# The opening of a two-layer trunk: the norm's row by a shuffle, weights ahead of tile two, tile two by VectorE, values ahead of keys

## The chip, the cores and the metric

The kernel runs on one core of one Trainium2 chip. The core has a matrix engine (TensorE, PE in the profile; its weight loads are PEld), a vector engine (VectorE, DVE), a scalar engine (ScalarE, ACT), GpSimd (POOL) and a sync engine (SyncE, SP) that here only issues loads and stores. PE writes into PSUM, everything else lies in SBUF, the on-chip memory, with 128 partitions. The metric is the device time of one execution in microseconds; the median over runs is what is compared.

## The reference

Two residual layers, each with one RMS norm, one wide input projection, three parallel token mixers (a Mamba-2 scan, sliding-window attention with sinks, forgetting attention) and one output projection, on 256 tokens of width 1024, all in float32. What matters here is how a layer begins:

```python
def rms_norm(x, w):
    xf = x.astype(jnp.float32)
    y = xf * lax.rsqrt(jnp.mean(xf * xf, axis=-1, keepdims=True) + NORM_EPS)
    return (y * w.astype(jnp.float32)).astype(x.dtype)
...
        h = rms_norm(x, norm_w[layer])
        proj = jnp.einsum('bsd,de->bse', h, w_in[layer])
...
    q = rope(q.reshape(b, s, SWA_HEADS, HEAD_DIM), cos, sin)
    k = rope(k.reshape(b, s, SWA_KV_HEADS, HEAD_DIM), cos, sin)
    v = v.reshape(b, s, SWA_KV_HEADS, HEAD_DIM)
```

The norm's weight `norm_w` is one row of 1024 numbers that multiplies every token. The first columns that the kernel projects are the 256 of the sliding window's keys (`b_k`) and the 256 of its values (`b_v`).

## The kernel before

**Tiling.** The 256 tokens are two tiles of 128 rows ("tile one" and "tile two"). A projection multiplies the transposed normalized tokens by a weight piece of 256 or 512 columns; the width of 1024 is cut into eight steps `k` of 128. To keep float32 accuracy with fast matmuls, each operand is split into a rounded part `hi` and a remainder `lo`, and each step is three matmuls: hi by hi, remainder of the tokens by hi, tokens by lo. So one tile by one piece is 24 matmuls.

**Weights.** SP loads the weights in parts of 512 KB into six buffers `raw` (`load_to`, line 345). ACT copies a part to `hi` (line 268, in the opening line 1209), then DVE subtracts to get `lo` (line 269; in the opening line 1210, where each part is done in two halves and POOL does the second half). A `raw` buffer is free for the next load once its `lo` is made; `hi` and `lo` have six buffers each and come free when PE has used the part. A 256-column piece is two parts, a 512-column piece four.

**The opening** is written out by hand in the first `manual_schedule` block, where each engine runs its instructions in program order. PE does 30 warm-up transposes. For each tile the sum of squares is built from two halves, `row_var` and `rsqrt` make the inverse root on DVE with one power on POOL (line 207), and the scaled row `h` is transposed by PE, four 128x128 blocks to a half, and split into `hTh` and `hTl` (`to_hT`). Tile one is scaled by DVE (line 1221). Tile two is multiplied by the norm's weight on POOL (1223, 1229) and by its inverse root on ACT (1235, 1237). Its transposes stand between the halves of the first 24 matmuls (`second_rows`). Then come keys of tile two, values of tile one, values of tile two (`u_bkv`): in all 96 matmuls of 256 columns. After a keys' unit DVE applies rope in three steps (474, 476, 477), POOL makes two sums (496), and a later step `rest` has PE transpose them and ACT evacuate (504).

**What follows** is written in an order that a planner sets from estimated PE time: the queries' piece of 512 columns for both tiles (`u_bq`, POOL's sums at line 517), a small piece, gate columns, and so on. `launch` gives a step a due time, and `pump`, called in the middle and at the end of units, issues the steps that are due. `layer_consts` issues nine small loads from ACT's queue (line 263): three into `vr`, four into `hb`, and two into `dsk` that gather `d_skip` element by element. SP and ACT loads share eight completion semaphores in turn, so a load can also wait for the load that last used its semaphore.

## Time and profile before

| what | value |
|---|---|
| median of 3 runs | 840.53 us (840.38 to 842.8) |
| profiled execution | 841.65 us |
| its span, first to last instruction | 839.8 us |
| mean granted TensorE clock | 0.997 |
| PE busy | 822.7 us, 98% of the span |
| loads: HBM read | 155.22 MB |

The span is what the profile covers; the execution's own time is 1.85 us longer. Rows of the profile give the start in microseconds, the duration, the engine, the line of the kernel, and the tiles written and read. A bracket at the end of a row is idle time of that engine just before it, with what ended the idle time. "ACTq" and "SPq" are the issuing of loads on those engines.

### The profile page before, as it was taken

The numbers are of one execution on the slowest core, as the hardware profiler recorded it, in microseconds if no ns is written. First come the engines' busy times: TensorE is split into PE (matmuls) and PEld (weight loads), VectorE is DVE, ScalarE is ACT, GpSimd is POOL, SyncE is SP. The second block draws the span as 40 slices with busy tenths as digits, with TensorE's granted clock in tenths as the row PEclk, the third lists the DMA queues.
The fourth block names the chain that finished last, engine by engine and source line by source line (L and its number), as shares of the span: only waits on it lengthen the run. The fifth ranks groups of instructions, "written<-read, shape, count | busy, mean of one in ns | idle before, by whom it ended". The sixth has DMA issues, their size and how long they took to land.

```text
span 839.8 us, 15652 instructions
## 1 busy us (share of the span) xinstructions
PE 822.7 (98%) x5800; PEld 749.8 (89%) x5800; DVE 655.9 (78%) x1355; ACT 503.3 (60%) x970; POOL 123.4 (15%) x167
## 2 busy tenths in 40 slices
PE   7999999999999999999999999999999999999996
PEld 6989888989989998888989998898899999888896
DVE  5778997998776678876688879979968668788665
ACT  6466777665556675544455668775556667655442
POOL 7411400000211101110014122000003110211000
PEclk9999999999999999999999999999999999999999
DMA  9576565567456546776577455556756564576632
GB/s 304 163 228 201 177 201 164 173 216 226 140 156 212 177 149 189 232 218 215 191 225 242 143 184 171 161 188 211 229 173 181 172 178 150 177 221 216 213 102 74
DMA packets 123595, 158.39 MB, mean 189 GB/s; under 512 B 12784, under 2 KB 84192, under 8 KB 123520
## 3 DMA queue, kind: packets, MB, share of 16 engines
q1 hardware_dynamic: 109456, 140.79, 53.9%
q10 hardware_dynamic: 14016, 16.49, 6.4%
q8 instruction: 45, 0.74, 0.4%
q14 instruction: 30, 0.25, 0.1%
q0 software_dynamic: 48, 0.13, 0.0%
HBM read 155.22 MB, written 2.16 MB: 187 GB/s over the span
## 4 chain that ended last, share of the span: by engine, by line
PE 82%; DVE 7%; DMA 4%; ACT 3%; issue 2%; POOL 1%; ACTq 1%; SPq 0%; POOLq 0%; DVEq 0%
PE mm L97 70%; PE mx L97 9%; DMA raw<-in_w_in_dram 4%; PE mx L101 3%; DVE lo L269 3%; ACT hi L268 1%; POOL sm L858 1%; DVE L L836 1%; DVE L L837 1%; DVE pp L577 1%; DVE pp L559 0%; ACT L L845 0%; ACTq L263 0%; ACT pp L565 0%; DVE L L842 0%
## 5 line engine op out<-in xcount | busy, mean ns | idle before, releaser
L269 DVE TENSOR_TENSOR lo<-raw,hi 128x1024 fp32r<-128x1024 f32 x252 | 310.8, 1247 | 77.4 <-ACT hi L268 71.9
L97 PE MATMUL mm<-hi,L 128*128 128x512 f32 (+1 forms) x1280 | 354.0, 363 | 1.8 <-ACT hi L1209 1.2
L97 PE MATMUL mm<-L,hi 128*128 128x256 f32 x1792 | 318.4, 279 | 0.9 <-DVE L L477 0.9
L268 ACT ACTIVATE hi<-raw 128x1024 fp32r<-128x1024 f32 x252 | 263.3, 1055 | 90.0 <-PE mm L97 68.3
L97 PEld LDWEIGHTS mm<-L,hi 128*128 128x128 f32 x1792 | 278.8, 193 | 6.9 <-issue 3.2
L97 PEld LDWEIGHTS mm<-hi,L 128*128 128x128 f32 x1280 | 229.2, 190 | 30.6 <-issue 2.4
L97 PE MATMUL mm<-L,lo 128*128 128x256 f32 x896 | 247.4, 276 | 0.0
L97 PE MATMUL mm<-lo,L 128*128 128x512 f32 (+1 forms) x640 | 229.4, 359 | 1.4 <-POOL lo L1210 1.4
L97 PEld LDWEIGHTS mm<-L,lo 128*128 128x128 f32 x896 | 172.7, 193 | 0.2
L97 PEld LDWEIGHTS mm<-lo,L 128*128 128x128 f32 x640 | 120.9, 189 | 15.4 <-POOL lo L1210 1.8
L908 POOL TENSOR_SCALAR_AFFINE_SELECT bias<-bias 128x128 f32<-128x128 f32 x64 | 37.3, 614 | 265.4 <-DMA bias<-cumd 265.3
L768 DVE SCALAR_TENSOR_TENSOR L<-L,vec,L 128x255 f32<-128x255 f32 (+2 forms) x96 | 46.9, 489 | 6.1 <-ACT L L765 4.8
L97 PE MATMUL mx<-L,L 128*64 128x128 f32 (+1 forms) x384 | 36.5, 332 | 0.0
L640 ACT ACTIVATE pp<-pp,nm 128x128 f32<-128x128 f32 x64 | 25.2, 394 | 15.6 <-DVE nm L633 12.6
L97 PEld LDWEIGHTS mx<-L,L 128*64 128x64 f32 x384 | 23.8, 137 | 11.9 <-issue 2.7
L565 ACT ACTIVATE pp<-pp,nm 128x128 f32<-128x128 f32 x64 | 28.2, 442 | 7.2 <-DVE nm L559 7.2
L932 ACT ACTIVATE L<-L 128x512 f32<-128x512 f32 x24 | 15.1, 627 | 29.0 <-DVE L L931 28.7
L829 ACT ACTIVATE L<-mm 128x256 f32<-128x256 f32 x48 | 18.0, 375 | 21.1 <-PE mm L97 17.4
L771 ACT ACTIVATE L<-L 128x256 f32<-128x256 f32 x32 | 13.4, 418 | 27.3 <-DVE L L768 26.9
L665 POOL TENSOR_SCALAR_AFFINE_SELECT L<-L 128x256 f32<-128x256 f32 x16 | 10.9, 680 | 107.7 <-ACT L L663 107.7
L633 DVE CUSTOM_DVE_ANT_0 pp<-mx,wmask,nsink 128x128 f32<-128x128 f32 x64 | 24.2, 413 | 1.8 <-PE mx L97 1.8
L858 POOL TENSOR_TENSOR sm<-sm,mhalf 128x4 f32<-128x4 f32 x8 | 10.9, 1363 | 91.8 <-DVE sm L855 91.8
(181 smaller groups left out, 820.8 us busy)
## 6 DMA issues: line engine op xcount, KB each, us to landing
raw<-in_w_in_dram SPq DMA_DIRECT2D x200, 512.0 KB, 4.7
raw<-in_w_proj_dram SPq DMA_DIRECT2D x48, 512.0 KB, 4.6
raw<-in_w_out_dram SPq DMA_DIRECT2D x16, 512.0 KB, 4.8
...
bias<-cumd ACTq DMA_DIRECT2D x16, 256.0 KB, 3.7
L<-in_gate_bias_dram ACTq DMA_DIRECT2D x12, 256.0 KB, 3.6
...
```

What stands on the lines that cost most here:

```text
L97: nc.tensor.matmul(o, a, b, **kw)
L101: nc.tensor.transpose(o, a, i)
L268: keep(act)(hi, src, AF.Copy)
L269: keep(tt)(lo, src, hi.bitcast(F32), op=ALU.subtract)
L565: act(pp[:, i, sl], pp[:, i, sl], AF.Exp, scale=-1.0, bias=nm[:, e:e + 1], accum_out=sums[:, e:e + 1])
L633: nc.vector.tensor_tensor_reduce(out=pp[:, i, sl], in0=score(p, i, b), in1=m, scale=-0.125, scalar=ns[:, i:i + 1], op0=ALU.add, op1=ALU.mi ...
L640: act(pp[:, i, sl], pp[:, i, sl], AF.Exp, scale=-1.0, bias=nm[:, e:e + 1], accum_out=sums[:, e:e + 1])
L768: stt(a[:, s:S], x_[:, 0:S - s], y.vec[:, 16 * j + u:16 * j + u + 1], a[:, s:S], op0=ALU.mult, op1=ALU.add)
L829: act(halves(th), p, AF.Tanh, scale=0.5)
L858: nc.gpsimd.tensor_tensor(r0[:, 0:4], v[:, 0:4], mhalf[:, 0:4], op=ALU.pow)
L908: nc.gpsimd.affine_select(out=bias[:, i, dst], in_=bias[:, i, src], compare_op=ALU.is_ge, fill=NEG, base=0, pattern=[[-1, P]], channel_mul ...
L932: act(g, g, AF.Tanh, scale=0.5)
```

## The change

Four things are changed, all in the opening.

- **The norm's row.** Before, SP loaded `norm_w` into all 128 partitions (512 KB). Now DVE clears a tile `nwr`, ACT issues a load of the row into four partitions (0, 32, 64 and 96; 16 KB), and two DVE shuffles spread partition 0 of each group of 32 over its group, into `nwb0`.
- **First weights ahead of tile two.** SP's order of loads was tile one, norm's weight, tile two, weights. It is now tile one, the first weight part, tile two, the other weights.
- **Tile two by DVE.** DVE now takes half of tile two's squares, and scales it in one step as it does tile one; both tiles are scaled in place. The POOL products and ACT scalings go. The inverse root is shorter by two DVE steps (`first_root`, `last_root`), and the first weight part's `lo` is made by DVE alone.
- **Values of tile one ahead of keys of tile two.** PE's order of units was keys one, keys two, values one, values two; it is keys one, values one, keys two, values two. Tile two's transposes now stand after keys one and in the middle of values one.

From there on the order on all engines is the same but for a few steps of the planner that move by some rows. The places of which the prediction speaks, as the instructions stand in program order:

On DVE, the first instructions before (ss is the sum of squares, sm and rs the small columns of the inverse root, L_22 the scaled tile one):

```order
L158 MEMSET tab_63 128x1
L1215 ISA L_26_154,ss_148<-L_2_66 128x512
L1215 ISA ss_148 128x1
L223 TENSOR_REDUCE sm_158<-ss_148 128x1
L224 TENSOR_SCALAR sm_158<-sm_158 128x1
L209 TENSOR_TENSOR sm_163<-sm_161 128x1
L210 TENSOR_TENSOR sm_163<-sm_163,sm_158 128x1
L211 TENSOR_SCALAR sm_163<-sm_163 128x1
L213 TENSOR_TENSOR rs_167<-sm_161,sm_163 128x1
L1221 SCALAR_TENSOR_TENSOR L_22_150<-L_2_66,rs_167,nwb_67 128x512 x2
```

And now (L_3 is the row's tile `nwr`, L_1 is x):

```order
L161 MEMSET L_3_66 128x1024
L164 MEMSET tab_69 128x1
L1252 STREAM_SHUFFLE nwb_64<-L_3_66 128x512 x2
L1226 ISA L_25_154,ss_150<-L_1_63 128x512
L1226 ISA ss_150 128x1
L241 TENSOR_SCALAR sm_160<-ss_150 128x1
L249 SCALAR_TENSOR_TENSOR sm_164<-sm_162,sm_160 128x1
L250 TENSOR_SCALAR sm_164<-sm_164 128x1
L252 TENSOR_TENSOR rs_167<-sm_162,sm_164 128x1
L1249 SCALAR_TENSOR_TENSOR L_1_63<-L_1_63,rs_167,nwb_64 128x512 x2
```

The shuffles, which read the loaded row, stand ahead of the squares of x; two of the small steps are gone.

On POOL, from the first power on, before (lo_237 and lo_262 are the values' weights, L_54 the sums of the rotated keys):

```order
L207 TENSOR_TENSOR sm_161<-sm_158,mhalf_96 128x1
L1223 TENSOR_TENSOR L_23_151<-L_2_66,nwb_67 128x512
L207 TENSOR_TENSOR sm_186<-sm_176,mhalf_96 128x1
L1210 TENSOR_TENSOR lo_195<-raw_105,hi_194 128x512
L1229 TENSOR_TENSOR L_23_151<-L_2_66,nwb_67 128x512
L1210 TENSOR_TENSOR lo_210<-raw_107,hi_209 128x512
L1210 TENSOR_TENSOR lo_237<-raw_109,hi_236 128x512
L1210 TENSOR_TENSOR lo_262<-raw_111,hi_261 128x512
L496 TENSOR_TENSOR L_54_273<-L_52_268,L_53_270 128x4x64 x2
```

And now (lo_229 and lo_233 are the values' weights):

```order
L243 TENSOR_TENSOR sm_162<-sm_160,mhalf_97 128x1
L243 TENSOR_TENSOR sm_193<-sm_191,mhalf_97 128x1
L1237 TENSOR_TENSOR lo_196<-raw_109,hi_195 128x512
L1237 TENSOR_TENSOR lo_229<-raw_111,hi_228 128x512
L511 TENSOR_TENSOR L_53_263<-L_51_258,L_52_260 128x4x64 x2
L1237 TENSOR_TENSOR lo_233<-raw_113,hi_232 128x512
L511 TENSOR_TENSOR L_59_331<-L_57_326,L_58_328 128x4x64 x2
```

The second half of the values' weights (lo_233) now stands behind the first keys' two sums; before, all weights' remainders stood ahead of them.

On PE, from tile one's last transposes to the first matmul of tile two's keys, before (L_24 and L_25 are hTh and hTl; hi_194 and hi_209 the keys' weights; mm_216 keys of tile one, mm_276 keys of tile two):

```order
L101 MATMUL mx_200<-ident_71,L_22_150 128x128 x4
L97 MATMUL mm_216<-hi_194,L_24_152 128x256 x4
L97 MATMUL mm_216<-hi_194,L_25_153 128x256 x4
L97 MATMUL mm_216<-lo_195,L_24_152 128x256 x4
L101 MATMUL mx_229<-ident_71,L_23_151 128x128 x4
L97 MATMUL mm_216<-hi_209,L_24_152 128x256 x4
L97 MATMUL mm_216<-hi_209,L_25_153 128x256 x4
L97 MATMUL mm_216<-lo_210,L_24_152 128x256 x4
L101 MATMUL mx_254<-ident_71,L_23_151 128x128 x4
L97 MATMUL mm_276<-hi_194,L_24_152 128x256
```

And now, from the second half of tile one's keys to the same place (L_23 and L_24 are hTh and hTl; hi_195 and lo_196 the keys' weights, hi_228, hi_232 and their lo the values'; mm_211 keys of tile one, mm_266 values of tile one, mm_301 keys of tile two):

```order
L97 MATMUL mm_211<-hi_195,L_23_152 128x256 x4
L97 MATMUL mm_211<-hi_195,L_24_153 128x256 x4
L97 MATMUL mm_211<-lo_196,L_23_152 128x256 x4
L101 MATMUL mx_248<-ident_72,L_1_63 128x128 x4
L97 MATMUL mm_266<-hi_228,L_23_152 128x256 x4
L97 MATMUL mm_266<-hi_228,L_24_153 128x256 x4
L97 MATMUL mm_266<-lo_229,L_23_152 128x256 x4
L101 MATMUL mx_279<-ident_72,L_1_63 128x128 x4
L97 MATMUL mm_266<-hi_232,L_23_152 128x256 x4
L97 MATMUL mm_266<-hi_232,L_24_153 128x256 x4
L97 MATMUL mm_266<-lo_233,L_23_152 128x256 x4
L97 MATMUL mm_301<-hi_169,L_23_152 128x256
```

Tile two's transposes (mx_248, mx_279) stand later, and the values' remainder lo_233 is needed ahead of the second tile's keys. On ACT the nine small loads of `layer_consts` stand right behind the evacuation of the first keys' transposes, in both kernels; the semaphores on which they and SP's weight loads wait are others.

The diff, without empty lines:

```diff
--- before.py
+++ after.py
@@ -154,14 +154,15 @@
             print("drained", br, left, "at", round(clock["t"], 1))
+    x0 = T("L8", [P, 2, D])
+    nwb0 = T("nwb", [P, D])
+    nc.sync.dma_start(x0[:, 0, :], x2[0:P, :])
+    nwr = T("L4", [P, D])
+    nc.vector.memset(nwr, 0.0)
+    nc.scalar.dma_start(nwr.rearrange("(a b) d -> a b d", b=32)[:, 0, :], norm_w[0:1, :].to_broadcast([4, D]))
     tab = T("tab", [P, 1])
     nc.vector.memset(tab, 0.0)
     act(tab, tab, AF.Exp)
-    x0 = T("L8", [P, 2, D])
-    nwb0 = T("nwb", [P, D])
-    nc.sync.dma_start(x0[:, 0, :], x2[0:P, :])
-    nc.sync.dma_start(nwb0, norm_w[0:1, :].to_broadcast([P, D]))
-    nc.sync.dma_start(x0[:, 1, :], x2[P:S, :])
     ident = T("ident", [P, P])
     make_identity(nc, ident)
     tri = T("tri", [P, P])
@@ -234,8 +235,22 @@
         stt(r[:, 0:1], a[:, 0:1], -3.0, r0[:, 0:1], op0=ALU.add, op1=ALU.mult)
         return r
-    def row_rstd(ss, n):
-        return rsqrt(row_var(ss, n), 1)
+    def first_root(ss):
+        v = T("sm", [P, 8])
+        ts(v[:, 0:1], ss[:, 0:1], ss[:, 1:2], 1.0 / D, op0=ALU.add, op1=ALU.mult)
+        r0 = T("sm", [P, 8])
+        nc.gpsimd.tensor_tensor(r0[:, 0:1], v[:, 0:1], mhalf[:, 0:1], op=ALU.pow)
+        return v, r0
+    def last_root(v, r0):
+        a = T("sm", [P, 8])
+        stt(a[:, 0:1], r0[:, 0:1], v[:, 0:1], r0[:, 0:1], op0=ALU.mult, op1=ALU.mult)
+        ts(a[:, 0:1], a[:, 0:1], -0.5, 1.5, op0=ALU.mult, op1=ALU.add)
+        r = T("rs", [P, 8], bufs=4)
+        tt(r[:, 0:1], r0[:, 0:1], a[:, 0:1], op=ALU.mult)
+        return r
@@ -1078,6 +1093,7 @@
             pump()
     fin = {}
+    between = []
     def hT(y, t):
         if t == 0:
@@ -1137,9 +1153,9 @@
         if l == 0:
             k, v = cols(C_BK), cols(C_BV)
-            op(k, u_bkv(y, 0, 0, [lambda j=j: second_rows(j) for j in range(2)]))
+            op(k, u_bkv(y, 0, 0, [lambda j=j: between[j]() for j in range(2)]))
             op(k, u_bkv(y, 0, 1))
-            op(v, u_bkv(y, 256, 0), u_bkv(y, 256, 1))
+            op(v, u_bkv(y, 256, 0, [lambda j=j: between[2 + j]() for j in range(2)]), u_bkv(y, 256, 1))
             op(None, lambda: layer_consts(y0))
             for c in (0, 2):
                 op(cols(C_BQ + 256 * c, 512), u_bq(y, c, 0), u_bq(y, c, 1))
@@ -1193,55 +1209,99 @@
     ENG = mybir.EngineType
     with tc.manual_schedule(engines={ENG.PE, ENG.DVE, ENG.Activation, ENG.Pool}):
+        load_to(1)
+        nc.sync.dma_start(x0[:, 1, :], x2[P:S, :])
         load_to(N_RAW)
         warm = pmx()
         for i in range(WARM):
             transpose(warm[:, 0:P], ident, ident)
         ss = [T("ss", [P, 4], bufs=4) for _ in range(2)]
-        h = [T("L4", [P, D]) for _ in range(2)]
         y0.hTh = T("L8", [P, NK // 2, 2, 2 * P], F32R)
         y0.hTl = T("L8", [P, NK // 2, 2, 2 * P], F32R)
-        def shared():
-            for _ in range(2):
-                raw, hi, lo = new_part()
-                for k, sub_ in ((0, tt), (2, gtt)):
-                    ks = slice(k, k + 2)
-                    act(hi[:, ks, :], raw[:, ks, :], AF.Copy)
-                    sub_(lo[:, ks, :], raw[:, ks, :], hi[:, ks, :].bitcast(F32), op=ALU.subtract)
-                yield
-        w0, w1 = shared(), shared()
         half = (slice(0, 512), slice(512, D))
         junk = T("L2", [P, 512])
-        nc.vector.tensor_tensor_reduce(out=junk, in0=x0[:, 0, half[1]], in1=x0[:, 0, half[1]], scale=1.0,
-                                       scalar=0.0, op0=ALU.mult, op1=ALU.add, accum_out=ss[0][:, 1:2])
-        sum_sq(x0, 0, 0, ss[0][:, 0:1], 512)
-        r0 = row_rstd(ss[0], 2)
-        sum_sq(x0, 1, 0, ss[1][:, 0:1], 512)
+        def squares(t):
+            sum_sq(x0, t, 0, ss[t][:, 0:1], 512)
+            nc.vector.tensor_tensor_reduce(out=junk, in0=x0[:, t, half[1]], in1=x0[:, t, half[1]], scale=1.0,
+                                           scalar=D * EPS, op0=ALU.mult, op1=ALU.add,
+                                           accum_out=ss[t][:, 1:2])
+        def part():
+            raw, hi, lo = new_part()
+            def high(k):
+                act(hi[:, k:k + 2, :], raw[:, k:k + 2, :], AF.Copy)
+            def low(k, sub_):
+                sub_(lo[:, k:k + 2, :], raw[:, k:k + 2, :], hi[:, k:k + 2, :].bitcast(F32), op=ALU.subtract)
+            return high, low
+        def turned(t, j):
+            p = pmx()
+            for k in range(4):
+                transpose(p[:, k * P:(k + 1) * P], x0[:, t, j * 512 + k * P:j * 512 + (k + 1) * P], ident)
+            pv = p.rearrange("p (a t) -> p a t", a=2)
+            h, l = y0.hTh[:, 2 * j:2 * j + 2, t, :], y0.hTl[:, 2 * j:2 * j + 2, t, :]
+            return (lambda: act(h, pv, AF.Copy)), (lambda: tt(l, pv, h.bitcast(F32), op=ALU.subtract))
+        def scaled(t, j, r):
+            stt(x0[:, t, half[j]], x0[:, t, half[j]], r[:, 0:1], y0.nwb[:, half[j]], op0=ALU.mult, op1=ALU.mult)
         for sl in half:
-            stt(h[0][:, sl], x0[:, 0, sl], r0[:, 0:1], y0.nwb[:, sl], op0=ALU.mult, op1=ALU.mult)
-        sum_sq(x0, 1, 512, ss[1][:, 1:2], 512)
-        gtt(h[1][:, half[0]], x0[:, 1, half[0]], y0.nwb[:, half[0]], op=ALU.mult)
-        v1 = row_var(ss[1], 2)
-        to_hT(h[0], 0, y0.hTh, y0.hTl, (0,))
-        r1 = rsqrt(v1, 1)
-        next(w0)
-        to_hT(h[0], 0, y0.hTh, y0.hTl, (1,))
-        gtt(h[1][:, half[1]], x0[:, 1, half[1]], y0.nwb[:, half[1]], op=ALU.mult)
-        def second_rows(j):
-            with tc.high_priority():
-                to_hT(h[1], 1, y0.hTh, y0.hTl, (j,))
-            next(w1)
-        act(h[1][:, half[0]], h[1][:, half[0]], AF.Copy, scale=r1[:, 0:1])
-        next(w0)
-        act(h[1][:, half[1]], h[1][:, half[1]], AF.Copy, scale=r1[:, 0:1])
-        for i, f, _ in ops[:2]:
-            f(pieces[i])
+            nc.vector.stream_shuffle(nwb0[:, sl], nwr[:, sl], [0] * 32)
+        squares(0)
+        r0 = last_root(*first_root(ss[0]))
+        h0, l0 = part()
+        h0(0)
+        h0(2)
+        scaled(0, 0, r0)
+        th0, tl0 = turned(0, 0)
+        scaled(0, 1, r0)
+        th0()
+        squares(1)
+        tl0()
+        th1, tl1 = turned(0, 1)
+        l0(0, tt)
+        root = first_root(ss[1])
+        h1, l1 = part()
+        h1(0)
+        th1()
+        h1(2)
+        l0(2, tt)
+        tl1()
+        r1 = last_root(*root)
+        l1(0, tt)
+        l1(2, gtt)
+        scaled(1, 0, r1)
+        scaled(1, 1, r1)
+        k0, k1, v0 = [f for _, f, _ in ops[:3]]
+        low = []
+        def next_parts():
+            load_to(N_RAW + 2)
+            for _ in range(2):
+                h, l = part()
+                h(0)
+                h(2)
+                low.append(l)
+        def turn_second(j):
+            th, tl = turned(1, j)
+            th()
+            low[j](0, tt)
+            tl()
+            low[j](2, gtt)
+        between.extend([next_parts, lambda: turn_second(0), lambda: turn_second(1), lambda: None])
+        k0(pieces[0])
+        v0(pieces[1])
+        k1(pieces[0])
         pieces[0].last = True
         release(pieces[0], 2)
-        run_op(*ops[2])
+        run_op(*ops[3])
     with tc.manual_schedule(engines={ENG.PE}):
-        for i, f, last in ops[3:]:
+        for i, f, last in ops[4:]:
             run_op(i, f, last)
```

## The prediction

> **What bounds the kernel now.** I read the page first, then stretches of the opening, then the chain of waits, then single rows of the opening in order of time.
>
> ```profile
> span 839.8 us, 15652 instructions
> PE 822.7 (98%) x5800; PEld 749.8 (89%) x5800; DVE 655.9 (78%) x1355; ACT 503.3 (60%) x970; POOL 123.4 (15%) x167
> ```
>
> TensorE (PE) is busy for 98% of the span, so a change to the opening can only move the start of an otherwise full row of matmuls. By stretch (duration after the colon, then busy time and count of each engine, granted clock, DMA share, GB/s):
>
> ```profile
> core 0: us, PE busy (x) PEld busy (x) DVE busy (x) ACT busy (x) POOL busy (x), PEclk, DMA share, GB/s
> 7.92:10.48 2.56, 1.31 (x8) 0.84 (x8) 1.68 (x5) 2.44 (x7) 2.23 (x2) 1.00 1.09 352
> 10.48:24.92 14.44, 12.99 (x104) 12.31 (x105) 11.00 (x19) 10.65 (x17) 12.52 (x9) 1.00 0.96 295
> 24.92:35.00 10.08, 10.08 (x53) 8.91 (x52) 6.34 (x12) 4.86 (x8) 2.25 (x3) 1.00 0.84 268
> 35.00:45.00 10.00, 10.00 (x52) 8.79 (x51) 7.82 (x17) 4.97 (x8) 3.83 (x4) 1.00 0.06 5
> 45.00:55.00 10.00, 9.48 (x73) 8.26 (x72) 5.56 (x9) 4.54 (x10) 1.41 (x1) 1.00 1.08 349
> ```
>
> From 24.92 to 45 PE has no gap. The keys-and-values stage (10.48 to 24.92) holds 104 matmuls and lasts 14.44 us, and this is what the change rebuilds. Note the fourth row: the weight stream is all but dead from 35 to 45 us. The chain of waits says why that matters (start, duration, what):
>
> ```profile
> 2.17 7.61 DMA raw<-in_w_in_dram
> 9.80 1.16 ACT hi L1209 x2
> 14.46 1.28 POOL lo L1210
> 16.73 7.03 PE mm L97 x60
> 23.80 1.32 DVE lo L269
> 25.14 5.80 DMA raw<-in_w_in_dram
> ...
> 31.82 0.65 ACTq L263
> ...
> 37.16 14.64 DMA raw<-in_w_in_dram
> ...
> 52.63 0.42 DVE L L474
> ...
> 55.36 2.95 PE mm L97 x24
> ...
> 71.05 2.68 PE mm L97 x24
> ```
>
> There are two bounds in turn. First the weights' landing (9.78), their split and GpSimd (POOL). Then, at 31.82, the d_skip loads of `layer_consts` go out, and a weight load issued at 37.16 lands only at 51.80, behind them. PE pays for that with the one gap after the opening (the bracket is idle time and its cause):
>
> ```profile
> 55.36 0.38 PE L97 MATMUL mm<-L,hi 128*128 128x256 f32 x1 [0.88 <-DVE L L477]
> ```
>
> So the end moves by the later of two shifts: that of the stage's end, and that of the weights behind the d_skip loads.
>
> **The parts, step by step.** The rows that carry the sum:
>
> ```profile
> 0.80 0.38 SPq L162 DMA_DIRECT2D L<-in_x_dram  x1
> 0.86 0.06 DVE L158 MEMSET tab<- 128x1 f32 x1 [0.86 <-PEq L1267]
> 0.93 0.20 POOL L168 MEMSET tri<- 128x128 f32 x1
> 1.52 5.33 PE L101 MATMUL mx<-ident 128*128 128x128 f32 x30 [1.52 <-POOL ident masks.py:199]
> 2.53 0.30 POOL L181 MEMSET wmask<- 128x256 f32 x1
> 4.42 0.69 DVE L1215 CUSTOM_DVE_ANT_0 L<-L 128x512 f32<-128x512 f32 x1 [3.50 <-DMA L<-in_x_dram]
> 5.23 0.15 DVE L223 TENSOR_REDUCE sm<-ss 128x1 f32<-128x2 f32 x1
> 5.42 0.15 DVE L224 TENSOR_SCALAR sm<-sm 128x1 f32<-128x1 f32 x1
> 7.12 1.42 DVE L1221 SCALAR_TENSOR_TENSOR L<-L,rs,nwb 128x512 f32<-128x512 f32 x2
> 7.92 1.32 PE L101 MATMUL mx<-ident,L 128*128 128x128 f32 x8 [1.08 <-DVE L L1221]
> 9.11 0.57 ACT L268 ACTIVATE L<-mx 128x512 fp32r<-128x512 f32 x1
> 10.48 1.50 PE L97 MATMUL mm<-hi,L 128*128 128x256 f32 x8 [1.24 <-ACT hi L1209]
> 10.97 0.69 DVE L1210 TENSOR_TENSOR lo<-raw,hi 128x512 fp32r<-128x512 f32 x1
> 14.46 1.27 POOL L1210 TENSOR_TENSOR lo<-raw,hi 128x512 fp32r<-128x512 f32 x1
> 18.70 0.41 DVE L474 TENSOR_TENSOR L<-mm,rope 128x256 f32<-128x256 f32 x1
> 25.88 0.57 ACTq L263 DMA_DIRECT2D vr<-in_conv_w_dram  x1
> 39.08 1.65 POOL L517 TENSOR_TENSOR L<-L,L 128x256 f32<-128x256 f32 x1 [5.55 <-DVE L L477]
> 43.02 1.46 POOL L517 TENSOR_TENSOR L<-L,L 128x256 f32<-128x256 f32 x2 [1.28 <-DVE L L477]
> ```
>
> *The norm's row.* The 512 KB broadcast leaves SP's queue, at 352 GB/s 1.5 us, so each weight part lands about that much sooner (the first, now ahead of tile two as well, by two loads: 9.78 becomes 6.8). In its place VectorE (DVE) clears 128x1024, then ScalarE (ACT) issues a 16 KB load, then DVE shuffles. No DVE clear of that size is in the trace; POOL's take 0.20 for 128 and 0.30 for 256 columns, so about 1.0 for 1024; it starts at 0.86 and the load goes out at about 1.95. Its flight is unknown. Nearest ends:
>
> ```profile
> out_dram<-L SPq DMA_DIRECT2D x2, 256.0 KB, 2.1
> vr<-in_conv_w_dram ACTq DMA_DIRECT2D x1, 32.0 KB, 5.1
> ```
>
> 2.1 with nothing beside it, 5.1 on this very queue behind a full weight stream: landing at 4.05 to 7.05. The stream is only filling at 2 us, so I take the flight of the x tile beside it (issued 0.80, its readers start at 4.42: 3.6), landing at 5.6. The shuffles are not in the trace either; the nearest rows for 512 columns on DVE are 0.69 and 0.71, and the ends are 0.5 and 0.71; I take 0.63, so both are done at S = 6.85.
>
> The shuffles stand ahead of DVE's squares, and they wait for the row. So DVE, which began on x at 4.42, now begins at S: what is queued behind that wait is the whole normalization, and PE waits for it.
>
> *Tile one's statistics.* From DVE's squares (4.42) to its first scaled half (7.12) was 2.70. The sum of squares and one product are fused away, two steps of 0.19 (5.23 to 5.42): 2.32. Scaling and transposes then run as before: first transpose at S+3.1 = 9.95 (7.92 before), the copy of 0.57 behind 0.6 of transposes, first multiply at S+4.35 = 11.2, against 10.48: **+0.7**. The earlier weights are hidden: ACT splits them by about 8, while x isn't ready.
>
> *Tile two by DVE.* Out go two POOL products and two ACT scalings; in come squares (0.70) and two scalings (0.68 each) on DVE, plus one `lo` half that POOL did. In DVE's order from S+3.67: squares to 4.4, lo of the transposed half to 5.1, two weight lo to 6.5, the other lo to 7.2, three small steps to 7.65, weight lo to 8.33, scalings to 9.7, weight lo to 10.3. PE's first 24 matmuls need 2.68 (row 71.05) but follow this list: they end at S+8.85, and tile two's transposes start with the first scaled half at S+9.06.
>
> *Values ahead of keys.* PE: transposes and twelve matmuls to S+10.95, transposes to 11.4, then ten of twelve to 12.6. The last two need the half of `lo` that POOL makes, and on POOL it now stands behind both sums of the rotated keys. Those wait for DVE's three rope steps (0.41 and two half as wide), which themselves wait behind tile two's lo: S+11.65. The sums take 0.73 each alone (row 43.02), 1.65 beside a DVE subtraction (row 39.08); one meets a half subtraction, so they end at 13.6; the lo takes 1.27: S+14.9. PE waits 2.3, the last two matmuls end at 15.15, and 48 more (twice 2.68) end the stage at S+20.5 = 27.35, against 24.92: **+2.4**, 0.7 of it from the start and 1.7 from a longer stage.
>
> *The rest of the opening.* Split weights of the queries still come in time by these steps: the first query `lo` ends at S+20, PE uses it at S+20.9. Costed at nothing; were DVE 1 us later, PE would wait that. SP's loads move with the buffers.
>
> *The d_skip loads.* The vectors' loads on ACT's queue (first at 25.88) stand behind the evacuation of the first keys' transposes, right after the stage, so the dead stretch moves with the stage, by 2.4. Two waits change. The second d_skip load now waits, by the shared semaphores, for the weight load whose buffer comes free with the third query `lo`; DVE ends that at S+22.9 = 29.8, where the chain has that load going out at 25.14, 4.6 later, of which the row at 31.82 hides all but some 0.5. And the weight load after next now waits for the third vector's landing, where it waited for loads long landed; if it is caught behind d_skip too, one more load of 1.5 us comes first at its end. Ends: -0.88, where PE's present wait is absorbed; +2.0 with both. I take **+0.7**, a third of the way from nothing to the upper end, and expect PE's gap near 58 us at about 1.6 instead of 0.88.
>
> Sum: +0.7 + 1.7 + 0.7 = **+3.1 us**. The profiled execution took 841.65 (span 839.8 and 1.85 around it), 1.1 over the median of 840.53; on that median the forecast is 843.6.
>
> **Weighed against the skill.** A first x tile of 3.6 us flight and the vectors' 5.1 speak for a queue that delays a newcomer. The Trainium skill, "DMA: Bandwidth & Descriptors", section on queues, rings and completion order, says that each engine takes the rings in turn packet by packet; by that the row wouldn't stand behind x, and the sum would be that of the first rival below. No row here shows a small load issued this early.
>
> **The rivals.**
> 1. *The row is early.* It lands at 4.05 like the idle-queue store: S = 5.3, stage end 25.8 (+0.9), d_skip +0.7: 842.1, within 0.3% (2.5 us, about what a measurement tells from no change). For: the stream has just begun. Against: the only ACT-queue row quoted took 5.1.
> 2. *The row is late.* It lands at 7.05 like the vectors: S = 8.3, stage end +3.9, and 0.7: 845.1. For: the same queue, and weights stand ahead on every engine by then. Against: only x and one or two loads do.
> 3. *The dead stretch decides in full.* Both waits bite: +2.4 and +2.0: 844.9. For: PE is already waiting there, so no slack. Against: with fewer weights in flight the vectors may land quicker.
> 4. *Faster, by the weights' landing.* If the chain's first rows bound alone, the 3.0 us by which the first weights land sooner go straight to the end: 837.5. It decides if the shuffles end before DVE's squares did begin (S near 4.4, landing by 3.2) and POOL's late lo is covered. For: 7.61 of landing stands first in the chain. Against: landing by 3.2 leaves a flight of 1.2, under every row.
> 5. *A slower clock.* PE idles from 6.85 (end of the 30 warm-up transposes) to 9.95, three times the 1.08 before. If the granted clock halved, the first 24 matmuls and their transposes would double by 3.6 us, 1.8 of which lies in time spent waiting: 845.4. Against: it stays 1.00 in every stretch quoted, through gaps of 1.2. The Trainium skill, "TensorE: Matmul & The Clock Gate", Part 1, gives an idle window of about 3.4 us for this, just over the gap forecast.
>
> **How the numbers follow.** Forecast 0.44; rivals, in their order, 0.24, 0.10, 0.10, 0.06, 0.06. The forecast's own range is 842.3 to 844.8 (landing half a microsecond to either side, d_skip 0 to 1.4); 0.3 of it lies under 843.05, the 0.3% line. Slower: 0.31 + 0.10 + 0.10 + 0.06 = 0.57. Same: 0.13 + 0.24 + 0.01 = 0.38. Faster: 0.05. The bounds of the unknown costs give 840.2 (landing 4.05, quick shuffles, the 0.88 absorbed) and 846.4 (landing 7.05, d_skip in full). The lower, three kind ends at once, is raised to 840.7, which leaves out the faster rival and a little more; the upper stands.
>
> **What would show it.** Shuffles starting at 5 to 6 us and DVE's squares behind them; first transposes near 10; a PE wait of about 2 us on POOL's lo near 20; stage end near 27; vector loads near 28.3, d_skip near 34.5, and PE's gap near 58 over 1 us. Wrong would be: shuffles before 4.4, POOL's lo ahead of PE, or a dead stretch that moves less than PE does.

## The result and the profile after

The changed kernel takes 849.48 us (median of 4 runs, 848.69 to 849.77) against 841.66 us for the kernel before on the same chip (840.38 to 843.25): 1.009 times as long, with a 95% interval of 1.0067 to 1.0113. It is slower, by more than twice the 3.1 us forecast, and lies over the top of the range (846.4). The profiled execution took 849.62 us. (Single executions of two repair kernels below, of 4852 and 1217 us, were disturbed; the comparisons leave them out.)

The page of the changed kernel, and TensorE's (PE's) waits over the whole span (total, how often, longest):

```profile
span 847.9 us, 15647 instructions
PE 824.8 (97%) x5800; PEld 751.5 (89%) x5800; DVE 661.5 (78%) x1361; ACT 501.8 (59%) x966; POOL 117.4 (14%) x164
...
PE mx L101 <- DVE L L1249: 4.8, 1, 4.8
PE mx L101 <- POOL L L532: 2.6, 3, 1.8
PE mx L97 <- DVE L L830: 1.9, 1, 1.9
PE mm L97 <- DVE lo L1237: 1.7, 1, 1.7
...
PE mm L97 <- POOL lo L1237: 1.3, 1, 1.3
```

PE makes the same 5800 matmuls; its busy time grew by 2.1 us, the span by 8.1, and the rest is waiting. The first row is the wait for tile one's scaled rows (1.08 us before); the second, on GpSimd's (POOL's) sums of the rotated queries, is new; the third, near 240 us, was 1.8 before; the last two are the stage's own. By stretch, from the first transposes to the end of the keys-and-values stage and on to 54 us:

```profile
core 0: us, PE busy (x) PEld busy (x) DVE busy (x) ACT busy (x) POOL busy (x), PEclk, DMA share, GB/s
12.21:14.01 1.80, 1.80 (x8) 1.57 (x8) 1.24 (x4) 0.65 (x2) 0.00 (x0) 0.50 1.03 379
14.01:32.53 18.52, 15.53 (x106) 15.00 (x106) 12.59 (x23) 10.59 (x17) 8.07 (x7) 0.83 0.48 124
32.53:42.00 9.47, 9.47 (x50) 8.38 (x49) 6.99 (x8) 1.81 (x3) 2.50 (x3) 1.00 0.66 208
42.00:54.00 12.00, 9.40 (x46) 7.54 (x46) 9.09 (x20) 6.00 (x10) 4.34 (x5) 1.00 0.42 116
```

The stage begins 3.5 us late (first multiply 14.01, was 10.48) and lasts 18.52 us, where it lasted 14.44; the clock starts at half. It ends at 32.53, 7.6 us late. Then PE loses 2.6 us between 42 and 54, where the kernel before lost nothing. The rows of the stage in order of time:

```profile
0.79 0.39 SPq L159 DMA_DIRECT2D L<-in_x_dram  x1
...
1.24 0.42 SPq L360 DMA_DIRECT2D raw<-in_w_in_dram  x1
...
1.71 0.50 SPq L1213 DMA_DIRECT2D L<-in_x_dram  x1
...
2.02 1.14 ACTq L162 DMA_DIRECT2D L<-in_norm_w_dram  x1
...
7.73 0.01 DVE L1252 LOAD_MASK_SELECT nwb<-L  x1 [5.73 <-DMA L<-in_norm_w_dram]
7.75 0.72 DVE L1252 STREAM_SHUFFLE nwb<-L 128x512 f32<-128x512 f32 x1
...
12.21 1.97 PE L101 MATMUL mx<-ident,L 128*128 128x128 f32 x8 [4.78 <-DVE L L1249]
...
16.39 2.54 POOL L1237 TENSOR_TENSOR lo<-raw,hi 128x512 fp32r<-128x512 f32 x2
16.52 1.18 DVE L249 SCALAR_TENSOR_TENSOR sm<-sm,sm 128x1 f32<-128x1 f32 x1
...
17.74 0.15 DVE L250 TENSOR_SCALAR sm<-sm 128x1 f32<-128x1 f32 x1
17.93 1.02 DVE L252 TENSOR_TENSOR rs<-sm,sm 128x1 f32<-128x1 f32 x1
...
19.61 0.77 PE L97 MATMUL mm<-lo,L 128*128 128x256 f32 x4 [1.74 <-DVE lo L1237]
...
25.34 1.25 POOL L1237 TENSOR_TENSOR lo<-raw,hi 128x512 fp32r<-128x512 f32 x1
26.64 0.49 PE L97 MATMUL mm<-lo,L 128*128 128x256 f32 x2 [1.25 <-POOL lo L1237]
```

Three things can be read here. VectorE (DVE) waits 5.73 us for the row, from 2.0 to 7.73. Two steps on 128 single numbers take 1.18 and 1.02 us while POOL makes two remainders; the step between them, which has one input, takes 0.15. And PE waits for the remainder behind them (1.74), then for POOL's (1.25). The rows behind the stage:

```profile
37.95 0.34 ACTq L278 DMA_DIRECT2D hb<-in_sinks_dram  x1
38.33 1.67 ACTq L278 DMA_DIRECT2D hb<-in_a_log_dram  x1
40.04 3.44 ACTq L278 DMA_DIRECT2D dsk<-in_d_skip_dram  x2
43.52 0.42 ACT L283 ACTIVATE L<-L 128x256 fp32r<-128x256 f32 x1 [9.05 <-DMA hb<-in_sinks_dram]
43.98 0.42 DVE L284 TENSOR_TENSOR L<-L,L 128x256 fp32r<-128x256 f32 x1 [4.46 <-ACT L L283]
...
45.99 0.44 PE L101 MATMUL mx<-ident,L 128*128 128x128 f32 x2 [1.85 <-POOL L L532]
```

The row at 43.52 is ScalarE's (ACT's) half of the split of the "small piece". It stands behind the nine vector loads, and these wait, by the shared semaphores, for weight loads: ACT computes nothing for 9.05 us. DVE's half of the split waits for it, and queued behind that on DVE stand the queries' rope, POOL's sum and PE's transposes.

### The profile page after: what moved, and what is told of

It is laid out like the page before. It is cut to its first block, busy times and chain, and to the rows that moved or that the text cites. A ratio compares the mean times of both kernels' runs of the same rounds, so it can differ in the third digit from the quotient of the medians.

```text
span 847.9 us, 15647 instructions
## 1 busy us (share of the span) xinstructions
PE 824.8 (97%) x5800; PEld 751.5 (89%) x5800; DVE 661.5 (78%) x1361; ACT 501.8 (59%) x966; POOL 117.4 (14%) x164
## 4 chain that ended last, share of the span: by engine, by line
PE 82%; DVE 8%; issue 3%; ACT 3%; DMA 2%; POOL 2%; POOLq 0%; ACTq 0%; DVEq 0%
PE mm L97 70%; PE mx L97 9%; DVE lo L284 3%; PE mx L101 3%; DMA raw<-in_w_in_dram 2%; ACT hi L283 1%; POOL sm L873 1%; DMA L<-in_norm_w_dram 1%; DVE L L851 1%; DVE L L852 1%; DVE pp L592 1%; DVE pp L574 0%; ACT L L860 0%; POOL lo L1237 0%; ACT pp L580 0%
## 5 line engine op out<-in xcount | busy, mean ns | idle before, releaser
L101 PE MATMUL mx<-ident,L 128*128 128x128 f32 x144 | 23.4, 288 | 7.4 <-DVE L L1249 4.8
L101 PEld LDWEIGHTS mx<-ident,L 128*128 128x128 f32 x144 | 17.8, 147 | 10.9 <-DVE L L1249 5.0
```

The costliest lines, as they stand in the source:

```text
L101: nc.tensor.transpose(o, a, i)
```

## The experiments

Two theories stood first: that the row's late landing is the cause (A), and that the rest of the change, by the way DVE, POOL and the order of the units hang together, makes the stage longer (R); the clock and the step behind the vector loads (D) are weighed beside them.

"Shift" is the start of the same matmul less its start in the kernel before, in the profiled executions: at the stage's end (24.92 before), in the next stretch (55.36 before), and at the end. The last two can differ by the second layer's own waits near 240 us, of which more below. The ratio is to the kernel before. A shift is of one execution: e9 and d1 leave all up to the stage's end as it is in the changed kernel, and their stages end at 32.16 and 32.34 where it had 32.53, so some 0.4 us there tell nothing. And of the kernels that keep the change only c1 has an interval apart from the changed kernel's; what a single repair does is read from the stage and its waits, not from the time.

| kernel | stage end | shift there | near 60 us | at the end | ratio (95%) |
|---|---|---|---|---|---|
| changed | 32.53 | +7.6 | +9.5 | +7.9 | 1.0090 (1.0067 to 1.0113) |
| e1 row undone | 29.38 | +4.5 | +5.8 | +6.4 | 1.0074 (1.0045 to 1.0103) |
| e2 row alone | 30.28 | +5.4 | +4.1 | +3.8 | 1.0073 (1.0045 to 1.0101) |
| e3 shuffles later | 30.60 | +5.7 | +7.0 | +6.2 | 1.0087 (1.0059 to 1.0115) |
| e4 long warm-up | 31.72 | +6.8 | +8.0 | +11.1 | 1.0134 (1.0109 to 1.0158) |
| e5 remainders on DVE | 30.77 | +5.9 | +7.2 | +9.9 | 1.0066 (1.0041 to 1.0091) |
| e6 row on SP's queue | 30.50 | +5.6 | +7.0 | +5.1 | 1.0069 (1.0045 to 1.0094) |
| e8 keys first | 33.86 | +8.9 | +9.6 | +9.2 | 1.0125 (1.0101 to 1.0150) |
| e9 small piece first | 32.16 | +7.2 | +8.3 | +8.3 | 1.0092 (1.0068 to 1.0117) |
| e10 tile two as before | 35.53 | +10.6 | +11.7 | +11.6 | 1.0135 (1.0102 to 1.0169) |
| d1 small piece, d_skip | 32.34 | +7.4 | +6.0 | +4.8 | 1.0074 (1.0050 to 1.0098) |
| c2b row repaired | 28.06 | +3.1 | +4.2 | +5.6 | 1.0064 (1.0036 to 1.0093) |
| c1 all repaired | 26.32 | +1.4 | 0.0 | -0.2 | 0.9988 (0.9971 to 1.0004) |
| b2 before, d_skip | 24.84 | -0.1 | -1.5 | -4.1 | 0.9974 (0.9957 to 0.9992) |
| b3 before, d_skip, row | 26.81 | +1.9 | +0.5 | -2.4 | 0.9979 (0.9964 to 0.9994) |

### The row undone, and the row alone

e1 is the changed kernel with SP's 512 KB broadcast again, ahead of the first weights:

```diff
-    nwr = T("L4", [P, D])
-    nc.vector.memset(nwr, 0.0)
-    nc.scalar.dma_start(nwr.rearrange("(a b) d -> a b d", b=32)[:, 0, :], norm_w[0:1, :].to_broadcast([4, D]))
+    nc.sync.dma_start(nwb0, norm_w[0:1, :].to_broadcast([P, D]))
...
-        for sl in half:
-            nc.vector.stream_shuffle(nwb0[:, sl], nwr[:, sl], [0] * 32)
```

> Only the norm's row is undone: SP again loads it into all partitions, behind tile one and ahead of the first weights; the rest of the change stays. Theory A (the row's late landing at 7.65 us, through DVE's order and then PE's clock, makes most of the 7.9 us): DVE's squares start near 4.5 instead of 9.0, the granted clock stays 1.00 from 10 to 25 us, the keys-and-values stage ends at 25 to 26 us instead of 32.5, and the time is 842 to 844. Rival R (the new order of the rest, values first and tile two on DVE, makes most of it): the stage ends past 29 us and the time stays at 846 or more.

e2 is the kernel before with this part alone put in.

> The kernel before with the row's part of the change alone: cleared tile, load of the row on ACT's queue, two shuffles ahead of DVE's squares. Theory A: squares start near 9 us, first transposes past 12, the clock halves in the stage, the stage ends at 28 to 30 us instead of 24.9, and the time is 844 to 847. Rival R: the row alone costs under 1.5 us (below 842.5), since weights and GpSimd hide it.

Neither part is the cause alone. With the row undone the transposes start at 7.73, yet the stage ends 4.5 us late; with the row alone it ends 5.4 late. Near 60 us the two (5.8 and 4.1) add to about the whole (9.5). In e1 tile two lands only at 9.9 us, behind the row and the first weights, and DVE waits 1.58 us for it: part of e1's 4.5 may be the order of the loads, which no run undoes alone.

### Where the row stands

e3 moves the two shuffles behind tile one's squares and root:

```diff
-        for sl in half:
-            nc.vector.stream_shuffle(nwb0[:, sl], nwr[:, sl], [0] * 32)
         squares(0)
         r0 = last_root(*first_root(ss[0]))
+        for sl in half:
+            nc.vector.stream_shuffle(nwb0[:, sl], nwr[:, sl], [0] * 32)
```

> The changed kernel with the two shuffles moved behind tile one's squares and inverse root on DVE; nothing else moves. Theory A1 (the wait stands in front of work that didn't need the row): the scaling starts near 9.0 instead of 11.4, PE's idle time before it falls from 4.8 to about 2.4 us, the clock stays near 1.00, and with 2.4 from the start and 2 from the clock the time is 844.5 to 846. Rival (the clock isn't the idle time's doing, or PE isn't bound there): only the 2.4 of the start or less, 847 to 849.

First transposes at 9.73, stage end 1.9 us sooner; the row still lands only at 7.7, so the shuffles begin there. The clock doesn't stay near 1.00 as expected (0.66 from 10 to 15 us), and the time, 848.39, is the rival's. e6 changes the queue of the load, and with it the order of SP's loads, since SP issues all later ones behind the row:

```diff
-    nc.scalar.dma_start(nwr.rearrange("(a b) d -> a b d", b=32)[:, 0, :], norm_w[0:1, :].to_broadcast([4, D]))
+    nc.sync.dma_start(nwr.rearrange("(a b) d -> a b d", b=32)[:, 0, :], norm_w[0:1, :].to_broadcast([4, D]))
```

> The changed kernel with the 16 KB row issued from SyncE's queue, right behind tile one of x, instead of from ScalarE's queue. SyncE then waits for VectorE's clear (until 1.97), so all later loads go out about 0.8 us later. Theory Q (the row is late because it goes as a newcomer on a second queue beside a full stream): it goes out near 2.0 and lands by 5.0, shuffles from 5.0 instead of 7.75, first transposes near 9.5 instead of 12.2, stage end near 30, 847. Theory L (a load of so few long rows takes its 5.6 us on any queue): shuffles at 7.5 or later, stage end 32.5 or later, 849.5 to 850.5.

In e6, in order of time:

```profile
0.79 0.38 SPq L159 DMA_DIRECT2D L<-in_x_dram  x1
...
2.02 0.66 SPq L162 DMA_DIRECT2D L<-in_norm_w_dram  x1
...
2.74 0.40 SPq L360 DMA_DIRECT2D raw<-in_w_in_dram  x1
...
5.11 0.01 DVE L1252 LOAD_MASK_SELECT nwb<-L  x1 [3.11 <-DMA L<-in_norm_w_dram]
```

Issued at the same moment, the same 16 KB is there after 3.1 us on SP's queue and after 5.7 on ACT's, though on SP's it pushes all later loads back. The forecasts of theory Q come true and theory L falls: the load isn't slow by itself. But two things differ. In the changed kernel SP has put out three loads of 512 KB before the row (0.79, 1.24 and 1.71); the last of them takes 5.7 us and so lands at 7.4, the row at 7.7, and the row's packets move only between 6.1 and 6.7. In e6 one such load stands ahead, which lands at 4.3, and the row at 5.1. So it is in all these runs: three loads ahead with the row on ACT's queue, one with it on SP's. Whether the queue or the loads ahead make the 2.6 us is therefore not shown. That the row lands close behind the loads put out before it, both times, speaks for these. The Trainium skill, "DMA: Bandwidth & Descriptors", section on queues, rings and completion order, has each engine take its queue rows in turn, packet by packet, which would let such a small newcomer through early; the 5.7 us here disagree, and the measurement decides.

### The clock

e4 warms up with 56 transposes instead of 30:

```diff
-WARM = 30
+WARM = 56
```

> The changed kernel with 56 warm-up transposes in place of 30, so that PE works to 10 us or more and idles some 2 us before tile one's transposes. Theory C (the 4.8 us of idle time drop the clock to half, and that lengthens the stage): granted clock 1.00 from 10 to 25 us where it was 0.50 to 0.82, stage end 1.5 to 2.5 us earlier than 32.5, time 847 to 848. Rival (DVE and GpSimd bind the stage, PE's clock is hidden): stage end within 0.5 us of 32.5, time 849 to 849.8.

From 10 to 15 us, first the changed kernel, then e4:

```profile
10.00:15.00 5.00, 2.79 (x12) 2.56 (x13) 3.56 (x9) 1.64 (x5) 0.57 (x1) 0.50 0.88 305
```

```profile
10.00:15.00 5.00, 3.28 (x20) 2.41 (x19) 4.02 (x12) 1.97 (x5) 0.57 (x1) 0.91 0.86 302
```

The granted clock is 0.91 in place of 0.50, and the stage ends 0.8 us sooner: the halved clock is real, and by this mostly hidden under waits. The clock isn't whole even so (0.75 from 15 to 20 us), and 0.8 is only twice what one execution tells from nothing. The total is longer all the same, 852.73, over both expected times, by the stretch near 240 us (shift 8.0 to 11.1).

### VectorE beside GpSimd

e5 gives the three half remainders that POOL makes in the opening to DVE:

```diff
-        l1(2, gtt)
+        l1(2, tt)
...
-            low[j](2, gtt)
+            low[j](2, tt)
```

> The changed kernel with the three half remainders that GpSimd makes in the opening made by VectorE instead. In the changed kernel two of VectorE's small steps of tile two's root take 1.18 and 1.02 us while GpSimd's remainders run (0.22 and 0.16 in other places), and TensorE later waits 1.25 us for the last of them. Theory R (VectorE is held up by GpSimd, and the order of the two sets the stage): the small steps come back to 0.25 or less, the wait of 1.25 us goes, VectorE has 2.0 us more of its own work but gains 1.8: the stage ends 1 to 2 us earlier (32.5 becomes 30.5 to 31.5), about 848.2. Theory A (only the row's landing and VectorE's list behind it count): the small steps shorten, but the 2.0 us of added work replaces them, stage end within 0.5 us of 32.5, 849.5.

The same small steps in e5:

```profile
16.55 0.21 DVE L249 SCALAR_TENSOR_TENSOR sm<-sm,sm 128x1 f32<-128x1 f32 x1
...
16.98 0.16 DVE L252 TENSOR_TENSOR rs<-sm,sm 128x1 f32<-128x1 f32 x1
```

1.18 and 1.02 became 0.21 and 0.16, and the stage ends 1.8 us sooner, though DVE has 2.0 us more to do. Theory R holds here. The 1.8 isn't the price of the two steps alone: PE's wait for POOL's remainder goes too, waits of 0.90 and 1.14 for DVE's remainders come in its place, and the clock from 20 to 25 us is 1.00 where the changed kernel has 0.66. The Trainium skill, "SBUF — State Buffer", section "Who interferes with whom", says that a DVE instruction with two inputs in SBUF contends with a GpSimd instruction that reads SBUF, that this is an exclusive lock, and that the order of issue decides who blocks. The trace agrees: 16.52 + 1.18 is 17.70, when POOL's first remainder ends by half of 2.54 (17.66), and the step with one input isn't held.

### The order of the units, and tile two

e8 puts keys of tile two ahead of values of tile one again:

```diff
-        between.extend([next_parts, lambda: turn_second(0), lambda: turn_second(1), lambda: None])
+        between.extend([lambda: (next_parts(), turn_second(0)), lambda: turn_second(1), lambda: None, lambda: None])
         k0(pieces[0])
-        v0(pieces[1])
         k1(pieces[0])
         pieces[0].last = True
         release(pieces[0], 2)
+        v0(pieces[1])
```

> The changed kernel with the first order of TensorE's units put back: keys of tile one, keys of tile two, values of tile one, values of tile two, with tile two's transposes between the halves of the first unit as before. Theory R (the order makes the stage longer): the 1.25 us wait for GpSimd's remainder behind the two key sums goes, since all remainders stand ahead of the sums; stage end 31.0 to 31.5 instead of 32.5, 848.3. Theory A (VectorE's list behind the late row sets the stage in any order): TensorE now waits for tile two's first scaled half in the middle of its first unit, 1 us or more, and the stage ends at 32 to 33, 849 to 850.

```profile
16.29 3.73 POOL L1237 TENSOR_TENSOR lo<-raw,hi 128x512 fp32r<-128x512 f32 x3
...
18.74 1.83 DVE L1237 TENSOR_TENSOR lo<-raw,hi 128x512 fp32r<-128x512 f32 x1
...
21.28 1.11 PE L101 MATMUL mx<-ident,L 128*128 128x128 f32 x4 [4.82 <-DVE L L1249]
```

PE waits 4.82 us for tile two in the middle of its first unit; values ahead of keys hides this. So that part of the change helps, by 1.3 us at the stage's end, once tile two is late. Theory R, as far as it blamed the order, falls; theory A had the direction, but put the stage's end at 32 to 33 and the time at 849 to 850, where they came at 33.86 and 852.62. Here a DVE remainder of normal length is held too (1.83 for 0.69).

e10 undoes the third part: tile two's squares and scaling on ACT, its product on POOL, the longer root, and half of the first weights' remainder on POOL. Its main lines:

```diff
-        squares(1)
+        sum_sq(x0, 1, 512, ss[1][:, 1:2], 512)
+        gtt(h2[:, half[0]], x0[:, 1, half[0]], y0.nwb[:, half[0]], op=ALU.mult)
...
-        scaled(1, 0, r1)
-        scaled(1, 1, r1)
+        act(x0[:, 1, half[0]], h2[:, half[0]], AF.Copy, scale=r1[:, 0:1])
+        act(x0[:, 1, half[1]], h2[:, half[1]], AF.Copy, scale=r1[:, 0:1])
```

> The changed kernel with its third part undone: tile two's squares on ScalarE, its product with the row on GpSimd and its scaling on ScalarE, the longer root, and half of the first weight part's remainder on GpSimd, all as in the kernel before; the row, the loads and values ahead of keys stay. Theory R3 (tile two's work on VectorE lengthens the stage): from first transposes to stage end 20.3 us falls to 18 or less (17.0 in the kernel before), stage end at 30.3 or sooner, 847.5 or less. Rival (what lengthens the stage is the late row and GpSimd's share, in either division): GpSimd's two products put its remainders and the second root later, TensorE waits for them instead; stage end 32 to 34, 849 to 851.

```profile
10.61 1.25 POOL L1265 TENSOR_TENSOR L<-L,nwb 128x512 f32<-128x512 f32 x1
10.66 1.22 DVE L249 SCALAR_TENSOR_TENSOR sm<-sm,sm 128x1 f32<-128x1 f32 x1 [0.77 <-POOL sm L243]
```

Worse by 3 us at the stage's end: POOL's product, released by the same late row, now holds even tile one's root. R3 falls: with tile two's work off DVE the stage is longer, not shorter. The time, 853.04, is over the rival's 849 to 851 too.

### The small piece, and d_skip

e9 moves the small piece's split back ahead of the vector loads, by giving it a high priority:

```diff
-            split(hi, lo, raw, keep=pin if state["pin"] else lambda f: f)
+            with tc.high_priority() if subs[stream[state["split"] - 1][0]][1] == 32 and state["split"] < 24 else __import__("contextlib").nullcontext(): split(hi, lo, raw, keep=pin if state["pin"] else lambda f: f)
```

> The changed kernel with one step moved: the split of the small piece (ScalarE's rounded part, VectorE's remainder) stands ahead of the nine vector loads on ScalarE's queue, as it did before, instead of behind them. Theory D (ScalarE, held by loads that wait for weights, holds that split, VectorE's rope behind it and so TensorE): TensorE's waits between 43 and 53 us (2.6 us, all on GpSimd's sums of the queries) go, and its shift against the kernel before stays at 7.6 us up to 42 to 52 us instead of rising to 10.8. Then there are two ends: if the weights behind the vector loads land in time, the end moves by 1.5 to 3 us, 846.5 to 848; rival (the vector loads' dead stretch decides in the end, in full): a new wait for weights or their remainder of 1 to 2.5 us appears between 52 and 62 us, and the end stays at 849 to 849.7.

The waits between 42 and 53 go. In their place stand two others:

```profile
61.56 1.19 PE L97 MATMUL mx<-L,qt 64*128 64x128 f32 x8 [0.95 <-ACT qt L541]
...
63.64 0.38 PE L97 MATMUL mm<-L,hi 128*128 128x256 f32 x1 [0.89 <-DVE L L492]
```

Together 1.84 us: DVE's rope there stands behind remainders of weights that land late. The end stays: the rival holds. d1 adds to e9, in both layers, one plain load of the d_skip row in place of the two that gather it:

```diff
-        y.hb = T("hb", [P, 64], bufs=2)
-        for i, v in enumerate((dt_bias, f_bias, sinks, a_log)):
+        y.hb = T("hb", [P, 80], bufs=2)
+        for i, v in enumerate((dt_bias, f_bias, sinks, a_log, d_skip)):
...
-        for half in range(2):
-            src = d_skip[l:l + 1, :].rearrange("o (j two) -> two o j", two=2)[half]
-            pdma(y.dsk[64 * half:64 * half + 64, :], src.to_broadcast([64, NK]))
+        for i in range(2):
+            pin(ts)(y.dsk[64 * i:64 * i + 64, :], y.hb[64 * i:64 * i + 64, 64:80].rearrange("p (j two) -> p two j", two=2)[:, i, :], 1.0, None, op0=ALU.mult)
```

> The changed kernel with the small piece's split ahead of the vector loads (as in e9) and, in both layers, the two element-by-element d_skip loads replaced by one plain row load beside the other four rows of hb, with two small VectorE copies later. Theory X (in e9 the d_skip loads took back what the split's move gave): e9's waits at 61.6 and 63.6 us (1.84 us together) go; the shift against the kernel before at 60 us falls from 8.3 to 6.0 to 6.6; and the wait of 1.9 us and the half-clock stretch of 3 to 4 us behind it, near 240 us where the second layer's d_skip loads go out, go too: 844 to 846.5. Rival Y (weights are late there because buffers come free late, with or without d_skip): one wait of 1 us or more stays near 62 us and near 245 us, and the time stays at 849 to 850.

Theory X holds near 60 us: both waits go, and the shift falls from 8.3 to 6.0. Near 240 it holds in part: a wait of 1.8 us stays, without the slow clock behind it. The ratio falls from e9's 1.0092 to 1.0074, less than expected. b2 is the kernel before with the same d_skip edit and nothing else:

> The kernel before with nothing changed but d_skip, in both layers: one plain row load in place of two element-by-element loads, and two small copies by VectorE. Theory X (the d_skip loads make the dead stretch of the weights): the wait of 0.88 us at 55 us goes, and near 240 us the wait of 1.8 us and the half-clock stretch behind it (granted 0.61 from 240 to 244): 836 to 838.5. Rival Y: the weights land no sooner, or another wait takes its place: 840 to 841.

The kernel before from 240 to 244 us, then b2's wait there:

```profile
240.00:244.00 4.00, 3.90 (x20) 3.52 (x21) 4.00 (x22) 3.32 (x15) 0.00 (x0) 0.61 0.05 0
```

```profile
PE mx L97 <- DVE L L814: 0.7, 1, 0.7
```

Before, the weight stream stands still there (DMA share 0.05) behind the second layer's d_skip loads; PE waits 1.8 us and then runs at a clock of 0.61. With plain rows the wait is 0.7, and the 0.88 at 55 us is gone. b2 is the fastest of these kernels: 838.25 us, 0.9974 of the kernel before (0.9957 to 0.9992).

### All repairs, and the row's alone

c1 is the changed kernel with the edits of e3 (the shuffles, though, between the power and the last root steps), e5, e6, e9 and d1 together:

> The changed kernel with every cause found so far taken away together: the row from SyncE's queue (e6), the shuffles behind tile one's squares (e3), all remainders on VectorE (e5), the small piece's split ahead (e9), d_skip as a plain row. If the causes add: first transposes near 8.3 (7.9 before, 12.2 in the changed kernel), stage 18.5 from there as in e5, its end at 26.5 to 27.5 (24.92 before), a shift of +1 to +2 us near 60 us, and 2 to 3.5 us back near 240 us: 838.5 to 841. Rival (the clock, or VectorE's list, holds the stage whatever the row does): stage end at 28.5 or later and 842 or more.

```profile
8.01:9.35 1.34, 1.31 (x9) 0.83 (x9) 1.23 (x4) 0.65 (x2) 0.00 (x0) 1.00 1.09 349
9.35:26.32 16.97, 14.10 (x104) 12.57 (x105) 12.88 (x26) 10.80 (x17) 4.33 (x4) 1.00 0.83 254
```

At the stage's end the repairs add, nearly: e3, e5 and e6 alone gave 1.9, 1.8 and 2.0 us, and c1 gives 6.2 (transposes at 8.01, stage end at 26.32). The time, 840.12 us, is that of the kernel before. The single repairs' gains in the ratio sum to 0.0064, c1's is 0.0102; the intervals are too wide to say whether more lies in that. c2 has the row's two edits alone, as they are in c1; c2b is the same kernel again, for its trace:

> The changed kernel with only the row repaired: issued from SyncE's queue (e6) and its shuffles behind tile one's squares (e3); GpSimd's remainders, the small piece and d_skip stay as in the changed kernel. If the causes add: first transposes near 8.0 as in c1, VectorE's two stretched small steps (1.2 and 1.0 us) and a wait of 1.2 to 2 us for GpSimd's remainder are there again, stage end at 28 to 28.5 (26.3 in c1), waits for GpSimd's sums of 2 to 3 us between 35 and 50 us, and 844 to 845.5. If the row is all that matters at the stage: stage end at 26.3 to 27, 842 to 843.5.

> The same kernel as c2_row_repairs, for its trace. If the causes add: first transposes near 8.0, small steps stretched, a wait of 1.2 to 2 us for GpSimd's remainder, stage end 28 to 28.5, waits for GpSimd's sums of 2 to 3 us between 35 and 50 us. By its first times (846 to 847) the stage end is rather 28.5 to 29.5.

Transposes at 8.25, small steps of 1.27 and 1.02, a wait of 2.00 for POOL's remainder, stage end 28.06, waits of 1.8 for POOL's sums later: as expected where the causes add, with the waits for the sums a little shorter; the time, 847.43 and 847.91, is over the 844 to 845.5 expected (ratios 1.0052 and 1.0064). So of the 6.2 us that c1 gives at the stage's end, the row's two edits give 4.5 and the remainders on DVE some 1.7. b3 asks whether a row spread by shuffles helps the kernel before at all; it is b2 with the row on SP's queue and the shuffles between variance and root:

```diff
+    nwr = T("L8", [P, D])
+    nc.vector.memset(nwr, 0.0)
+    nc.sync.dma_start(nwr.rearrange("(a b) d -> a b d", b=32)[:, 0, :], norm_w[0:1, :].to_broadcast([4, D]))
...
-    nc.sync.dma_start(nwb0, norm_w[0:1, :].to_broadcast([P, D]))
...
-        r0 = row_rstd(ss[0], 2)
+        v0 = row_var(ss[0], 2)
+        for sl in half:
+            nc.vector.stream_shuffle(nwb0[:, sl], nwr[:, sl], [0] * 32)
+        r0 = rsqrt(v0, 1)
```

> The kernel before with the plain d_skip row (b2), and the norm's row by 16 KB on SyncE's queue and two VectorE shuffles, which stand between tile one's variance and its root; nothing else of the change. Theory W (the weights' landing bounds the first matmul): the first weight part lands 1 us or more sooner, the first matmul moves from 10.4 to 9.7 to 10.0 though the transposes move from 7.95 to 8.3, stage end 24.2 to 24.5, 837.5 to 838. Rival (VectorE's 1.3 us of shuffles come back in its remainders and in the start): first transposes at 8.5 or later, stage end 25 or later, 838.5 to 839.5.

```profile
6.64 1.27 POOL L1227 TENSOR_TENSOR L<-L,nwb 128x512 f32<-128x512 f32 x1 [0.48 <-DMA L<-in_x_dram]
6.78 1.14 DVE L212 TENSOR_TENSOR sm<-sm,sm 128x1 f32<-128x1 f32 x1
```

It doesn't: PE's wait for the weights halves (ACT's hi, 1.1 to 0.5), but transposes start at 9.15 and the stage ends at 26.81. The shuffles push a root step to where POOL's product, for tile two, holds it, and the clock is 0.63 from 10 to 15 us. The rival holds.

## Why the prediction was wrong

Right were the sign, and which instruction waits for what: the whole normalization behind the row, then the values' last matmuls behind POOL's late remainder. By the prediction's steps:

- **The norm's row** failed by its flight. The clear took 0.91 (forecast about 1.0), the load went out at 2.02 (1.95), the shuffles follow each other by 0.63 (0.63). The flight took 5.7, not 3.6, and over the upper end of 5.1: squares start at 8.99, not 6.85. The 3.6 were x's, which went out on SP's queue with nothing ahead of it. Ahead of the row stood x and two more loads of 512 KB; at the prediction's own 1.5 us for each, behind x's landing at 4.4, the last lands at 7.4, as it did, and the row came 0.3 later. Rival 2 had the thought ("weights stand ahead on every engine by then") at a chance of 0.10, with squares from 8.3; its row of ACT's own queue, 5.1, was nearly right. Its stage end, +3.9, fell short all the same, by the steps below.
- **Tile one's statistics** held: transposes at S+3.2 (forecast 3.1). The first multiply came at S+5.0, not S+4.35, by the half clock.
- **Tile two by DVE** failed in one term: "three small steps" counted 0.45 us; they took 2.4 (16.52 to 18.95), held beside POOL's remainders: 2.0 more. PE's wait of 1.74 is for the remainder right behind them.
- **Values ahead of keys** held as a mechanism: PE waits for the remainder behind the sums, 1.25 us where 2.3 were forecast, since PE comes late itself.
- **Rival 5, the clock**, came true on top: PE idles 4.8 us, and the clock is 0.50. What e4 takes back is 0.8 us, with the clock not yet whole, against the 1.8 priced. The argument against it, a clock of 1.00 through gaps of 1.2, left out the stretch near 240 us, where the kernel before itself ran at 0.61 behind a wait of 1.8. The Trainium skill, "TensorE: Matmul & The Clock Gate", Part 1, puts the halved clock after an idle window of about 3.4 us; the gap of 4.8 agrees, the 0.66 from 20 to 25 us, behind a wait of 1.74, doesn't.
- **The rest of the opening, costed at nothing**, failed. The order of the changed kernel has the small piece's split behind the nine vector loads; the text ahead of the prediction named "a few steps of the planner that move by some rows", and the prediction didn't ask what such a step stands behind. Waits of 2.6 us came of it.
- **The d_skip loads** were right as a mechanism and unseen in the result: PE, late by then, meets no gap near 60 us. Once the split is moved back, the waits are 1.84 us (e9; forecast 1.6), and plain rows take them away (d1).

The stage's end was forecast at 27.35 and came at 32.53, 5.2 us later. Of these, 2.1 are the later start of the squares; in the rows, 2.0 more come with the held small steps, and the rest, some 1.1, goes mostly to the halved clock, as far as e4 shows (0.8). The runs that undo one cause each give 2.0 (e6), 1.8 (e5) and 0.8 (e4), but these are no separate prices: e5 and e6 change the clock as well, and e5 a second wait. Behind the stage 1.8 us were added, in place of 0.7.

What stays open: whether the queue or the loads ahead made the row late, and how the runs' scatter arises. With the old d_skip loads the shift at the end differs from that near 60 us by -1.9 to +3.1 from kernel to kernel, in the profiled executions, through the wait and the half clock near 240 us. That this depends on when PE arrives there is an inference.
